# One step of a hybrid decoder layer on one core: q's opening, the widths of the product passes, and the products that follow a norm

## The chip, the core and the metric

The kernel runs on one core of a Trainium2 chip. Five engines work side by side: TensorE (PE in the profile, with PEld for its weight loads), VectorE (DVE), ScalarE (ACT), GpSimd (POOL) and SyncE (SP), which here issues nearly all DMAs. Each executes its own list of instructions in order; semaphores order them among each other. The metric is the time of one execution on the device, in microseconds (us).

## What is computed

One layer, applied to a prompt of 256 positions and to 8 samples of 4 new positions, 288 rows in all, in float32:

```
h   = RMSNorm(x)                                      x: 288 x 2048
q, k, v, u, v_g = split(h @ w_in)                     5 x 1024 columns; q and k with a partial rotary
A   = block-sparse attention (top 3 past blocks by q . mean(k), and the own block)
      the samples' past: 8 x 2048 positions in a paged cache of keys and values
B   = gelu(u) * (tril(W_s) @ LayerNorm(gelu(v_g)) + b)     in chunks of 128 positions
mix = (sigmoid(h Wg_a) * (A Wa) + sigmoid(h Wg_b) * (B Wb)) @ w_o
x   = x + RMSNorm(mix)
x   = x + RMSNorm((silu(a1) * g1) @ w_ffn_out),   a1, g1 = split(RMSNorm(x) @ w_ffn_in)    hidden width 5632
y   = x + (p @ w_ple) * sigmoid(RMSNorm(x) @ w_ple_gate)
```

## The kernel before, in words

**Layout.** Activations are kept transposed: a feature tile is 128 features on the partitions and T = 288 rows along the free dimension; x has KD = 16 tiles. A float32 product is made of three matmuls in a reduced float32 form. Weights are split into a high part `wh` (ScalarE, L224) and a low part `wl` (VectorE, L225), activations likewise into a pair of 288 + 288 columns (hh and hl in `hhl`, zh and zl in `zhl`, and so on). L228 multiplies wh with the high part, L229 wh with the low part, L230 wl with the high part.

**`product`** (L210) makes 256 output columns (two tiles t, two accumulators) over n feature tiles. It goes in chunks of four tiles k: one DMA of 512 KB into `wr` (WR = 4 buffers), a cast, a subtraction (three buffers each of wh and wl), then 24 matmuls ordered by (tile k, output tile t). In a chunk of fewer than four the order is by output tile first. With `wide` = 32 the first pass covers 320 columns, the second 256, and the 32 columns beyond T are added at the end through a small tile `rest` (L234, L235); with `wide` = 0 all three passes have 288. Only w_ffn_out's products set `wide`. A product is a generator that yields after each chunk; `weave` advances two of them in a given proportion.

**Opening** (L136 to L264). x comes in four DMAs of four tiles on SP's queue, q's weights beside them; gains and c_mix on ACT's queue, cst, the page table and kcst on POOL's. Ten matmuls on constants wake PE. Two of q's four products run together chunk by chunk as x arrives, behind them the sum of squares and `r0` (`r0_of`), the inverse root mean square of x. r0 multiplies the results of the products, not their inputs, so it is needed only at the first eviction. The other two products of q follow (L773). `rope` (L275) evicts q and k: a multiplication with r0 and four steps on 32 rows.

**Cache stage.** k, v, v_g, u and the gates' products follow, and the paged keys and values are scored between them. Every page is a DMA of 512 KB, preceded on SP by a read of its number in the page table (`page_load`, L553). Three big tiles of four pages each can be in flight; the first twelve pages can therefore be loaded before any score is made. In this stage, up to w_gate's last product, there are three "acc", two "long" and three "aux" banks of PSUM; afterwards six "acc" and two "aux".

**After the two norms.** mix and the FFN's output are normalised over all features: `norm_gap` puts small products of p with w_ple on PE while the norm's factor is computed. `residual` (L921) then walks over x in pairs of tiles: scale (L933), add to x (L935), split into zh (L937) and zl (L938), square (L940), add the squares up (L942, VectorE). The three first products of w_ffn_in, and of w_ple_gate, are woven in steps of chunks (L985, L1026); the residual as a whole stands ahead of them in the program. Their evictions need the factor of the next norm (r2, r3), which needs all squares.

**Tail.** Each product of w_ple_gate ends in four steps a tile (L1018 to L1021) and one DMA of two tiles to y.

**Order.** The order on each engine is not written out: a scheduler lists the instructions by their place in the program and by its own estimate of when their inputs are ready. `tc.issue_after(i)` forces an instruction behind another.

Of the kernel before, what the change touches and what calls it, by code (L numbers as in the profile page):

```python
# [42 lines left out]
WAKE, WR, BIG, PT, AUX, PB, LEAD, EG, LE, N1, N2, REST = 10, 4, 3, 1, 3, 2, 6, 2, 4, 20, 38, 325.0  # L43
# [40 lines left out]
def drain(gen):  # L84
    for _ in gen:
        pass
# [22 lines left out]
def tile_hybrid_step(ctx: ExitStack, tc: tile.TileContext, a: dict, o: list):  # L109
# [26 lines left out]
    def x_load(c):  # L136
        nc.sync.dma_start(xs[c], a["x"][:, c * XK:c * XK + XK])
# [17 lines left out]
    nc.gpsimd.dma_start(kcst, a["c_perm"][:, 128:])  # L155
# [30 lines left out]
    def h_parts(c):  # L186
        for i in range(XK):
            k = c * XK + i
            nc.scalar.activation(hh[:, k], xs[c][:, i], AF.Copy, scale=g_pre[:, k:k + 1])
            nc.vector.scalar_tensor_tensor(hl[:, k], xs[c][:, i], g_pre[:, k:k + 1], hh[:, k], op0=ALU.mult, op1=ALU.subtract)  # L190
# [16 lines left out]


    def product(w, c0, ks, part, done, name, of="acc", wide=0, hold=()):
# [4 lines left out]
        for k0 in range(0, n, 4):  # L214
            m = min(4, n - k0)
            raw = perm.tile([128, 4, GC], F32, name="wr", bufs=WR)
            r0 = ks[k0] * 128
            nc.sync.dma_start(raw[:, :m], w[r0:r0 + m * 128, c0:c0 + GC].rearrange("(k p) c -> p k c", p=128))
# [7 lines left out]
            for i, t in [(i, t) for i in range(m) for t in range(2)] if m == 4 else [(i, t) for t in range(2) for i in range(m)]:  # L226
# [4 lines left out]
            yield 0.74 * m  # L231
# [16 lines left out]
    def q_gen(g, of="acc"):  # L248
        yield from product(w_in, g * GC, K16, hpart, lambda x: rope(qT[:, 2 * g:2 * g + 2], x), "q", of)
# [14 lines left out]
    nc.scalar.dma_start(cm, a["c_mix"])  # L264
# [508 lines left out]
    for q in q2 + [q_gen(2), q_gen(3)]:  # L773
        drain(q)
# [306 lines left out]
```

## Time and profile before

| | us |
|---|---|
| median of 3 runs (lowest, highest) | 1820.64 (1820.21, 1822.02) |
| the profiled execution | 1820.68 |
| its span, first to last instruction | 1818.9 |

| Engine | busy us | share of the span |
|---|---|---|
| PE | 1798.5 | 99% |
| VectorE | 951.9 | 52% |
| ScalarE | 769.2 | 42% |
| GpSimd | 90.6 | 5% |

The granted TensorE clock is 0.996 of full on average. The DMA queues move 414.81 MB, 228 GB/s over the span; in the cache stage, up to about 700 us, they move 340 to 365 GB/s, afterwards about 165. Since matmuls are pipelined and their ends modelled, a busy PE tells nothing of its pace: a stage in which PE never stops is read by its number of matmuls and its length. Names in the rows such as fa, fg, f, o, pg are the accumulators of w_ffn_in's two halves, w_ffn_out, w_o and w_ple_gate.

### The profile page before, as it was taken

To read this page: it belongs to the slowest core of one execution; us is meant where nothing else is said; L and a number is where in the kernel's file an instruction comes from. 1 tells how busy PE (TensorE), PEld (TensorE's weight loads), DVE (VectorE), ACT (ScalarE), POOL (GpSimd) and SP (SyncE) were. 2 spreads that over 40 slices of the span, in tenths; PEclk is the share of its full clock that TensorE was granted. 3 is DMA by queue.
4 is the path that set the end of the run, shared out by engine and by line. 5 is a ranking of instruction groups with operands and counts; after the bars stand their busy time and mean duration, and the time that the engine had idled before them with its cause. 6 is when DMAs were issued, how large, how long until landed. Compare 5 with 4: busy or idle time off the path is not lost.

```text
span 1818.9 us, 38387 instructions
## 1 busy us (share of the span) xinstructions
PE 1798.5 (99%) x15818; PEld 1752.1 (96%) x15818; DVE 951.9 (52%) x1363; ACT 769.2 (42%) x1081; POOL 90.6 (5%) x169
## 2 busy tenths in 40 slices
PE   7999999999999999999999999999999999999998
PEld 7999899999999989999999999999999999999998
DVE  6654447544344346544854555434455554444774
ACT  5334465444333344445533333333333333444642
POOL 1010112000000000011000000000000000011000
PEclk9999999999999999999999999999999999999999
DMA  9589999999999995555555555455555555546363
GB/s 345 163 280 367 323 360 337 365 350 359 352 345 368 358 321 201 170 164 161 152 169 166 163 167 169 157 168 165 172 165 172 163 164 170 165 158 195 122 196 112
DMA packets 309136, 414.81 MB, mean 228 GB/s; under 512 B 13120, under 2 KB 273344, under 8 KB 308832
## 3 DMA queue, kind: packets, MB, share of 16 engines
q1 hardware_dynamic: 307728, 409.16, 67.0%
q8 instruction: 124, 2.03, 0.5%
q0 software_dynamic: 944, 2.79, 0.4%
q10 hardware_dynamic: 288, 0.41, 0.1%
q14 instruction: 52, 0.43, 0.1%
HBM read 407.45 MB, written 4.85 MB: 227 GB/s over the span
## 4 chain that ended last, share of the span: by engine, by line
PE 94%; DVE 3%; DMA 1%; SPq 1%; issue 1%; ACT 1%; DVEq 0%; ACTq 0%
PE f L228 6%; PE f L230 5%; PE fg L228 5%; PE fg L230 5%; PE fg L229 5%; PE fa L230 5%; PE fa L228 5%; PE fa L229 5%; PE f L229 5%; PE values L696 3%; PE scores L598 3%; PE gb L228 2%; PE ga L228 2%; PE gb L230 2%; PE o L228 2%; PE o L230 2%
## 5 line engine op out<-in xcount | busy, mean ns | idle before, releaser
L225 DVE TENSOR_TENSOR wl<-wr,wh 128x1024 fp32r<-128x1024 f32 x512 | 618.8, 1209 | 708.2 <-ACT wh L224 704.4
L224 ACT CAST wh<-wr 128x1024 fp32r<-128x1024 f32 x512 | 530.9, 1038 | 881.0 <-PE f L229 140.4
L228 PE MATMUL f<-dhl,wh 128*128 128x320 f32 x704 | 217.1, 308 | 0.0
L229 PE MATMUL fg<-zhl,wh 128*128 128x288 f32 x704 | 208.2, 296 | 0.0
L230 PE MATMUL fa<-zhl,wl 128*128 128x288 f32 x704 | 206.8, 295 | 1.2 <-DVE wl L225 1.2
L229 PE MATMUL fa<-zhl,wh 128*128 128x288 f32 x704 | 207.9, 296 | 0.0
L228 PE MATMUL fg<-zhl,wh 128*128 128x288 f32 x704 | 207.3, 295 | 0.2 <-ACT wh L224 0.2
L230 PE MATMUL fg<-zhl,wl 128*128 128x288 f32 x704 | 207.0, 295 | 0.0
L230 PE MATMUL f<-dhl,wl 128*128 128x288 f32 x704 | 207.0, 294 | 0.0
L228 PE MATMUL fa<-zhl,wh 128*128 128x288 f32 x704 | 206.3, 296 | 0.1
L229 PE MATMUL f<-dhl,wh 128*128 128x256 f32 x704 | 196.6, 279 | 0.0
L230 PEld LDWEIGHTS fa<-zhl,wl 128*128 128x128 f32 x704 | 133.3, 189 | 1.4 <-DVE wl L225 1.4
L230 PEld LDWEIGHTS fg<-zhl,wl 128*128 128x128 f32 x704 | 133.3, 190 | 0.0
L229 PEld LDWEIGHTS f<-dhl,wh 128*128 128x128 f32 x704 | 132.4, 188 | 0.0
L228 PEld LDWEIGHTS fg<-zhl,wh 128*128 128x128 f32 x704 | 132.1, 188 | 0.4 <-ACT wh L224 0.4
L229 PEld LDWEIGHTS fa<-zhl,wh 128*128 128x128 f32 x704 | 132.4, 188 | 0.1
L229 PEld LDWEIGHTS fg<-zhl,wh 128*128 128x128 f32 x704 | 132.3, 188 | 0.0
L228 PEld LDWEIGHTS fa<-zhl,wh 128*128 128x128 f32 x704 | 131.6, 188 | 0.7 <-ACT zhl L937 0.4
L230 PEld LDWEIGHTS f<-dhl,wl 128*128 128x128 f32 x704 | 132.2, 188 | 0.0
L228 PEld LDWEIGHTS f<-dhl,wh 128*128 128x128 f32 x704 | 132.0, 188 | 0.0
L228 PE MATMUL gb<-hhl,wh 128*128 128x288 f32 x256 | 76.7, 300 | 0.0
L228 PE MATMUL ga<-hhl,wh 128*128 128x288 f32 x256 | 76.5, 299 | 0.0
(327 smaller groups left out, 3740.6 us busy)
## 6 DMA issues: line engine op xcount, KB each, us to landing
wr<-in_w_ffn_in SPq DMA_DIRECT2D x176, 512.0 KB, 3.7
kt<-in_cache_k SPq DMA_DIRECT2D x128, 512.0 KB, 7.7
vt<-in_cache_v SPq DMA_DIRECT2D x128, 512.0 KB, 6.6
wr<-in_w_in SPq DMA_DIRECT2D x80, 512.0 KB, 7.2
wr<-in_w_ffn_out SPq DMA_DIRECT2D x80, 512.0 KB, 3.4
wr<-in_w_gate SPq DMA_DIRECT2D x64, 512.0 KB, 7.4
wr<-in_w_o SPq DMA_DIRECT2D x32, 512.0 KB, 3.5
wr<-in_w_ple_gate SPq DMA_DIRECT2D x32, 512.0 KB, 3.5
```

Of the source, the lines that this page charges most:

```text
L224: nc.scalar.copy(wh[:, :m], raw[:, :m])
L225: nc.vector.tensor_tensor(wl[:, :m], raw[:, :m], wh[:, :m], ALU.subtract)
L228: nc.tensor.matmul(accs[t], wh[:, i, c], x[:, :T + wide], start=k == 0, stop=False)
L229: nc.tensor.matmul(accs[t][:, wide:T], wh[:, i, c], x[:, T + wide:], start=False, stop=False)
L230: late["mm"] = nc.tensor.matmul(accs[t][:, :T], wl[:, i, c], x[:, :T], start=False, stop=k == n - 1)
L598: i = nc.tensor.matmul(sp[b][32 * g:32 * g + 32, 4 * n:4 * n + 4], Q[:, h2, g, dq], kt[:, :, c:c + 32], start=h2 == 1 and dq == 0, stop=h2 ...
L696: i = nc.tensor.matmul(oa[b][32 * g:32 * g + 8], w[:, n, 32 * g + 8 * part:32 * g + 8 * part + 8], v[:, :, g], start=first and part == 3, ...
```

## The change

- **Opening.** x comes in pieces of tiles (0,1), (1,2), (2,4), (4,8), (8,12), (12,16), the second on ACT's queue. Three products of q run together over these pieces, in banks "acc", "long" and "aux"; for pieces of fewer than four tiles the weights have buffers of their own (`w1`, `w2`). `r0_of` now stands ahead of the third product's last chunk, behind the last matmul before it. cst, kcst and c_mix move to SP's queue, behind weight loads 11 and 13. Each of the first twelve pages (FIRST) is issued only after weight load 9 + n. Eight wake matmuls in place of ten.
- **Products.** `wide` is 32 everywhere: passes of 320, 256 and 288 columns. The last chunk of every product is ordered by output tile first.
- **After the norms.** The first three products yield after each tile (`fine`), and `first_products` advances the residual by one pair for every two tiles of the first product, four tiles ahead at the start. The squares' sums are taken out of the residual's loop and made in one go (`norm_of_squares`) once all pairs have been put out.
- **Tail.** The last tile's four steps are made in two halves of 144 columns, and the last two tiles of y have a DMA each.

```diff
-WAKE, WR, BIG, PT, AUX, PB, LEAD, EG, LE, N1, N2, REST = 10, 4, 3, 1, 3, 2, 6, 2, 4, 20, 38, 325.0
+WAKE, FIRST, WR, BIG, PT, AUX, PB, LEAD, EG, LE, N1, N2, REST = 8, 12, 4, 3, 1, 3, 2, 6, 2, 4, 20, 38, 325.0
...
-    def x_load(c):
-        nc.sync.dma_start(xs[c], a["x"][:, c * XK:c * XK + XK])
+    pieces = [(0, 1), (1, 2), (2, 4)] + [(k, k + XK) for k in range(XK, KD, XK)]
+
+    def x_load(k0, k1):
+        (nc.scalar if k0 == 1 else nc.sync).dma_start(xs[k0 // XK][:, k0 % XK:k0 % XK + k1 - k0], a["x"][:, k0:k1])
...
-    x_load(0)
+    x_load(*pieces[0])
+    x_load(*pieces[1])
     cst = perm.tile([128, 128], F32, name="cst")
-    nc.gpsimd.dma_start(cst, a["c_perm"][:, :128])
...
-    nc.gpsimd.dma_start(kcst, a["c_perm"][:, 128:])
...
-    def product(w, c0, ks, part, done, name, of="acc", wide=0, hold=()):
+    def product(w, c0, ks, part, done, name, of="acc", wide=32, cuts=None, hold=(), fine=False):
...
-        for k0 in range(0, n, 4):
-            m = min(4, n - k0)
-            raw = perm.tile([128, 4, GC], F32, name="wr", bufs=WR)
+        for k0, k1 in cuts or [(k, min(k + 4, n)) for k in range(0, n, 4)]:
+            m = k1 - k0
+            if cuts and m < 4:
+                raw = p_x0.tile([128, m, GC], F32, name=f"w{m}", bufs=6 // m)
+            else:
+                raw = perm.tile([128, 4, GC], F32, name="wr", bufs=WR)
...
-            for i, t in [(i, t) for i in range(m) for t in range(2)] if m == 4 else [(i, t) for t in range(2) for i in range(m)]:
+            steps = [(i, t) for i in range(m) for t in range(2)]
+            for i, t in sorted(steps, key=lambda s: s[1]) if k1 == n else steps:
...
-            yield 0.74 * m
+                if fine and t and k1 < n:
+                    yield 0.74
+            if not fine or k1 == n:
+                yield 0.74 * m
...
-    q2 = [q_gen(0), q_gen(1, "long")]
-    for c in range(KD // XK):
-        h_parts(c)
-        for q in q2:
+    q3 = [q_gen(g, of, pieces) for g, of in enumerate(("acc", "long", "aux"))]
+    for i, (k0, k1) in enumerate(pieces):
+        h_parts(k0, k1)
+        for q in q3:
+            if k1 == KD and q is q3[2]:
+                squares(k1 // XK - 1)
+                with tc.issue_after(late["mm"].ins):
+                    r0_of()
             next(q)
-        if c + 1 < KD // XK:
-            x_load(c + 1)
-        squares(c)
-    r0_of()
+        if 1 < i + 1 < len(pieces):
+            x_load(*pieces[i + 1])
+        if k1 % XK == 0 and k1 < KD:
+            squares(k1 // XK - 1)
+    with tc.issue_after(loads[11].ins):
+        nc.sync.dma_start(cst, a["c_perm"][:, :128])
+        nc.sync.dma_start(kcst, a["c_perm"][:, 128:])
...
-    nc.scalar.dma_start(cm, a["c_mix"])
+    with tc.issue_after(loads[13].ins):
+        nc.sync.dma_start(cm, a["c_mix"])
...
+            if len(issued) < FIRST:
+                st.enter_context(tc.issue_after(loads[9 + len(issued)].ins))
...
-            if m:
-                nc.vector.tensor_tensor(src[:, 0:2], src[:, 0:2], src[:, s], ALU.add)
+            yield
+
+    def norm_of_squares(src, key):
+        for m in range(2, KD, 2):
+            nc.vector.tensor_tensor(src[:, 0:2], src[:, 0:2], src[:, m:m + 2], ALU.add)
         ssq[key] = [src[:, 0], src[:, 1]]
+        return norm_of(key)
+
+    def first_products(ps, src, rstd, g_next):
+        res = residual(src, rstd, g_next)
+        drain(islice(res, 2))
+        for i, _ in enumerate(weave(weave(ps[0], 1.0, ps[1], 1.0), 2.0, ps[2], 1.0)):
+            if i % 2:
+                next(res, None)
+            if i == 11:
+                yield
...
-            drain(weave(weave(pairs[0], 1.0, pairs[1], 1.0), 2.0, pairs[2], 1.0))
+            first = first_products(pairs[:3], mo_f, r1, g_pf)
+            next(first)
+            r2 = norm_of_squares(mo_f, "x1")
...
+            drain(first)
...
-            nc.vector.tensor_tensor(gt, x[t], r3, ALU.mult)
...
+            for c in (slice(0, T // 2), slice(T // 2, T)) if m == KD - 1 else (slice(0, T),):
+                nc.vector.tensor_tensor(gt[:, c], x[t][:, c], r3[:, c], ALU.mult)
...
+            if g == 7:
+                nc.sync.dma_start(y_o[:, m], x1[:, m])
```

## Rows read from the trace of the kernel before

**Rows 1.** The page, part 1: engine, busy us (share of span), instructions.

```profile
PE 1798.5 (99%) x15818; PEld 1752.1 (96%) x15818; DVE 951.9 (52%) x1363; ACT 769.2 (42%) x1081; POOL 90.6 (5%) x169
```

**Rows 2.** View of waits, PE: what waited for what; us, times, longest.

```profile
PE q L228 <- ACT wh L224: 6.3, 2, 3.8
PE q L230 <- DVE wl L225: 2.5, 3, 1.6
...
PE fa L230 <- DVE wl L225: 1.2, 1, 1.2
```

**Rows 3.** Timeline of PE: start us, us, instruction, count, [idle before <- releaser].

```profile
9.54 0.61 PE L228 MATMUL q<-hhl,wh 128*128 128x288 f32 x1 [3.84 <-ACT wh L224]
...
72.47 0.29 PE L228 MATMUL k<-hhl,wh 128*128 128x288 f32 x1
```

**Rows 4.** Windows of w_o, w_ffn_in, w_ffn_out: length, busy (count) by engine, clock, DMA.

```profile
750.00:846.00 96.00, 96.00 (x728) 96.00 (x727) 41.58 (x38) 45.70 (x65) 14.92 (x13) 1.00 0.56 180
...
1275.00:1555.00 280.00, 280.00 (x2114) 280.00 (x2113) 141.47 (x174) 108.58 (x135) 0.00 (x0) 1.00 0.54 167
1562.00:1696.00 134.00, 134.00 (x1018) 134.00 (x1017) 62.40 (x81) 61.71 (x95) 16.93 (x13) 1.00 0.55 175
```

**Rows 5.** Timeline of SP's issues in the opening.

```profile
1.21 0.97 SPq L218 DMA_DIRECT2D wr<-in_w_in  x2
...
25.36 4.98 SPq L560 DMA_DIRECT2D kt<-in_cache_k  x4
31.60 6.26 SPq L218 DMA_DIRECT2D wr<-in_w_in  x4
```

**Rows 6.** DMA view from 0.5, 12, 31, 52: KB, us to landing.

```profile
x<-in_x SPq DMA_DIRECT2D x1, 576.0 KB, 4.6
...
DMA packets 3533, 7.40 MB, mean 390 GB/s; under 512 B 219, under 2 KB 2275, under 8 KB 3532
...
wr<-in_w_in SPq DMA_DIRECT2D x3, 512.0 KB, 9.8
...
wr<-in_w_in SPq DMA_DIRECT2D x4, 512.0 KB, 3.6
```

**Rows 7.** Window 45 to 50 us; after POOL's come clock, DMA share and GB/s.

```profile
45.00:50.00 5.00, 5.00 (x21) 5.00 (x22) 2.89 (x3) 0.50 (x2) 0.00 (x0) 0.50 0.65 189
```

**Rows 8.** Timeline of ACT and DVE, 5 to 9 us.

```profile
5.52 1.81 ACT L189 ACTIVATE hhl<-x,gains 128x288 fp32r<-128x288 f32 x4 [2.83 <-DMA gains<-in_gains]
...
7.26 0.43 DVE L567 COPY spread<-cst 128x512 f32<-128x512 f32 x1 [6.25 <-DMA cst<-in_c_perm]
```

**Rows 9.** Groups of DVE by line, 28 to 72.4 us: busy us, mean ns.

```profile
L278 DVE TENSOR_TENSOR A<-q,r 128x288 f32<-128x288 f32 x7 | 2.9, 450 | 1.2 <-PE q L230 1.2
...
L281 DVE TENSOR_TENSOR rope<-rope,cm 32x576 f32<-32x576 f32 x3 | 2.2, 744 | 0.1
```

**Rows 10.** View of tile rest, 1270 to 1700 us: ns min/median/max.

```profile
L234 ACT COPY rest<-f x18: 172/174/187, 1279.6 to 1699.7; 128x32 f32<-128x32 f32 x18
L235 DVE TENSOR_TENSOR f<-f,rest x18: 191/193/200, 1280.9 to 1699.9; 128x32 f32<-128x32 f32 x18
```

**Rows 11.** Groups of DVE by line, 854.3 to 889 us.

```profile
L225 DVE TENSOR_TENSOR wl<-wr,wh 128x1024 fp32r<-128x1024 f32 x9 | 11.0, 1228 | 0.0
L938 DVE SCALAR_TENSOR_TENSOR zhl<-x,gains,zhl 128x288 fp32r<-128x288 f32 x16 | 8.1, 520 | 0.1
...
L942 DVE TENSOR_TENSOR mo_f<-mo_f 128x576 f32<-128x576 f32 x7 | 5.3, 761 | 0.0
```

**Rows 12.** Timeline of ACT behind the first norm.

```profile
866.44 2.95 ACT L224 CAST wh<-wr 128x1024 fp32r<-128x1024 f32 x3 [0.63 <-ACT mo_f L940]
```

**Rows 13.** Timeline of DVE and SP in the tail.

```profile
1812.93 0.85 DVE L1018 TENSOR_TENSOR pgt<-pg,r_x 128x288 f32<-128x288 f32 x2 [6.90 <-PE pg L230]
...
1815.52 0.36 SPq L1022 DMA_DIRECT2D out<-x  x1
```

**Rows 14.** Window of u's products in the cache stage.

```profile
325.00:397.00 72.00, 72.00 (x843) 67.18 (x842) 36.95 (x70) 30.92 (x43) 4.08 (x13) 1.00 1.02 365
```

More of the change, by code (lines that the diff above doesn't have):

```diff
@@ L771, in cache_gen @@
         products()
-    for q in q2 + [q_gen(2), q_gen(3)]:
+    for q in q3 + [q_gen(3)]:
         drain(q)
@@ L919, in tile_hybrid_step, with residual @@
     zh, zl = zhl[:, :, :T], zhl[:, :, T:]
-    def residual(src, rstd, g_next, key):
+    def residual(src, rstd, g_next):
         last, adds = [], []
@@ L982, in tile_hybrid_step @@
             hold = [late["sq"]] if half == 0 and g == 1 else []
-            pairs += [product(w_fi, c0, K16, zpart, done_a, "fa", hold=hold), product(w_fi, FF + c0, K16, zpart, done_g, "fg")]
+            pairs += [product(w_fi, c0, K16, zpart, done_a, "fa", hold=hold, fine=half == 0 and g < 2),
+                      product(w_fi, FF + c0, K16, zpart, done_g, "fg", fine=half == 0 and g < 1)]
         if half == 0:
-            drain(weave(weave(pairs[0], 1.0, pairs[1], 1.0), 2.0, pairs[2], 1.0))
+            first = first_products(pairs[:3], mo_f, r1, g_pf)
+            next(first)
+            r2 = norm_of_squares(mo_f, "x1")
+            end_m.close()
+            p_f, end_f = pool("p_f", "left")
+            dhl = p_f.tile([128, HT, 2 * T], F32R, name="dhl", tag="dh")
+            dh, dl = dhl[:, :, :T], dhl[:, :, T:]
+            fo = p_f.tile([128, KD, T], F32, name="fo")
+            drain(first)
         for p in pairs:
@@ L1017, in pg_done @@
             gt = p_f.tile([128, T], F32, name="pgt", tag="fs", bufs=4)
-            nc.vector.tensor_tensor(gt, x[t], r3, ALU.mult)
-            nc.scalar.activation(gt, gt, AF.Sigmoid)
-            nc.vector.tensor_tensor(gt, gt, le[:, m], ALU.mult)
-            nc.vector.tensor_tensor(x1[:, m], x1[:, m], gt, ALU.add)
-        nc.sync.dma_start(y_o[:, 2 * g:2 * g + 2], x1[:, 2 * g:2 * g + 2])
-    pg = [product(w_pg, g * GC, K16, zpart, lambda x, g=g: pg_done(x, g), "pg",
-                  hold=[late["sq"], late["fo"]] if g == 2 else []) for g in range(8)]
-    drain(weave(weave(pg[0], 1.0, pg[1], 1.0), 2.0, pg[2], 1.0))
+            for c in (slice(0, T // 2), slice(T // 2, T)) if m == KD - 1 else (slice(0, T),):
+                nc.vector.tensor_tensor(gt[:, c], x[t][:, c], r3[:, c], ALU.mult)
+                nc.scalar.activation(gt[:, c], gt[:, c], AF.Sigmoid)
+                nc.vector.tensor_tensor(gt[:, c], gt[:, c], le[:, m, c], ALU.mult)
+                nc.vector.tensor_tensor(x1[:, m, c], x1[:, m, c], gt[:, c], ALU.add)
+            if g == 7:
+                nc.sync.dma_start(y_o[:, m], x1[:, m])
+        if g < 7:
+            nc.sync.dma_start(y_o[:, 2 * g:2 * g + 2], x1[:, 2 * g:2 * g + 2])
+    pg = [product(w_pg, g * GC, K16, zpart, lambda x, g=g: pg_done(x, g), "pg",
+                  hold=[late["sq"], late["fo"]] if g == 2 else [], fine=g < 3) for g in range(8)]
+    first = first_products(pg[:3], fo, r4, g_pl)
+    next(first)
+    r3 = norm_of_squares(fo, "x2")
+    drain(first)
     for p in pg[3:]:
```

28 lines of the change are left out of this document (10 added, 18 removed).

## The prediction

> **What bounds the kernel now.** I first read the page's busy shares: TensorE (PE) is busy 99% of the span [rows 1]. So I ask two things only: where PE still waits, and at what pace it streams. The view of waits, PE alone, answers the first: in 1818.9 us PE waits 8.8 us in q's opening and 1.2 us where w_ffn_in begins after a norm (the same again where w_ple_gate begins); the other waits are under 1.2 us each [rows 2]. Two stretches don't show up there in full: the time before q's first matmul at 9.54 us [rows 3], and the tail after the last matmul. The windows answer the second question: in the stages of w_o, w_ffn_in and w_ffn_out PE never stops, so a stage's time is the number of its matmuls times their pitch [rows 4].
>
> The profiled execution took 1820.68 us (span 1818.9 and 1.8 around it), the median of three runs is 1820.64; so the sum is made against 1820.68 and needs no correction.
>
> **Opening, the largest term.** q's 384 matmuls and the 4 of r0 run from 9.54 us to k's first at 72.47 [rows 3], 62.9 us. At the pitch of w_o's window, (728 - 2)/96 us or 132.2 ns each [rows 4], 384 take 50.8 and r0's about 0.8; 11.3 us are lost inside, 9.5 before. The loss inside: the twelve first pages of the cache (kt) stand in one queue with q's weights. SP issues four kt loads from 25.36 us, and the first weights of q's third product only at 31.60 [rows 5]; these need 9.8 us to land, 3.6 when the queue is short [rows 6]. PE then waits for a cast of those weights and for their low part (6.3 and 2.5 us with the start [rows 2]), and after these waits the granted clock is 0.50 from 45 to 50 us, the lower of its two levels [rows 7].
>
> The change does four things to it.
> (a) The first piece needs one tile of x (144 KB) and weight pieces of 128 KB in place of 576 and 512. Now x needs 4.6 us from its issue at 0.76 to landing [rows 6], gains are there at 5.52, and VectorE stands at `spread` until 7.26, waiting for `cst`, with hl behind it [rows 8]. With `cst` behind load 11, `spread` can't hold up hl at 7 us; should it stand in VectorE's order ahead of `cst`'s landing, it holds up a wl later, which I price with the losses below. One tile of x lands 432 KB or 1.1 us (at 390 GB/s [rows 6]) sooner, at 4.2; gains between that and 5.5. I take 5.0. Then hh 0.45 (a quarter of 1.81 [rows 8]), hl about 0.5 (zl, the same form, has 0.52 [rows 11]; the 320-column pass reads both), and hops: first matmul at 6.0, ends 5.2 and 7.0. Two wakes fewer end the wake sooner, for an opening that starts sooner.
> (b) Three products use each tile of x, so PE has more work to each byte of x; and page n now stands behind load 9 + n, one page to a load. In the stretch of loads 9 to 17 come 9 loads, 9 pages, half of x and 0.65 MB of constants: 18 x 0.524 + 1.18 + 0.65 = 11.3 MB, 29 us at the 390 GB/s that the queue gave when it was full [rows 6]. PE's work on these loads is 216 x 0.1322 = 28.6 us. The queue keeps pace with no slack but its head start: 0.5 us of waits, with 0 and 6 as ends.
> (c) More DMAs are issued: 9 pieces of weights and 6 of x for what took 5 loads and 4 of x. SP issues two in 0.97 us [rows 5], so eight extra are 4 us of SP, spread over 13 us of PE's work on the pieces: piece 1 is issued by 3.6 us, and PE wants it at 8.4. The smaller casts carry a fixed share each: bounded by a quarter and two fifths of a four-tile cast (1.0 to 1.2 us [rows 11, 12]) ACT and VectorE have at most 3 x 0.5 + 0.5 = 2.0 us for a tile, against PE's 18 x 0.132 = 2.4. The second and third casts still come one after the other at the start: 1.5 us. POOL loses two issues and ACT one; SP's three for constants stand behind loads 11 and 13, ahead of pages and later loads, and their bytes are in the sum of (b).
> (d) r0 now comes at the end: its matmuls stand behind the second product's last, and rope of all three products waits for it. A rope is 2 x 0.45 + 4 x 0.74 = 3.9 us on VectorE [rows 9], 11.7 for three; q's last product needs 4 wl of 1.2 us in the same 13 us. That is 16.6 us of work on an engine that runs in order, and a wl queued behind rope makes PE wait: 0 (two wl are done before r0) to 3.6; I take 1.5.
> Sum: 6.0 + 50.8 + 0.8 + 0.5 + 1.5 + 1.5 = 61.1 us for 72.5: **-11.4 us**, ends -5 and -15. Everything behind starts relative to q's end, pages too, so the shift is kept.
>
> **Passes of 320, 256, 288.** Still three matmuls and 864 columns; but w_ffn_out has these widths already. Its window gives (1018 - 2) in 134 us, 131.9 ns a matmul; w_ffn_in's (2114 - 2) in 280, 132.6; w_o's 132.2 [rows 4]. So 0.7 ns on 4224 matmuls of w_ffn_in, 3.0 us, and about 0.35 on the other 5760, 2.0 us: **-5.0 us**, ends 0 and -7. Each of 112 products gains two copies of 0.17 us on ACT and two adds of 0.19 on VectorE [rows 10], about 40 us on either; in w_ffn_in's window they are busy 109 and 141 of 280 us [rows 4], so it costs PE nothing while a bank is free. The last chunk tile by tile gives the first accumulator 1.6 us (12 matmuls) more for that and moves no work: 0.
> By the Trainium skill (TensorE: Matmul & The Clock Gate, Back-to-back issue gap) a warm matmul costs its columns at 2.4 GHz and 2.5 ns more, so three passes of 864 columns cost the same however they are cut, and this term would be 0. The trace's 132.2 ns for 288 columns lies 9.7 above that figure, so something else is in the pitch, and the rule need not hold for it; its result is rival B.
>
> **Products woven after the two norms.** From 854 to 889 us VectorE has no gap: 9 wl (11.0 us), 16 zl (8.1), 7 adds of squares (5.3), and the residual's scalings and sums [rows 11]. Three woven products use up their three wh buffers together, so casts for all three start in a row at 866.44 [rows 12], and the first wl behind them stands after such adds. PE loses about 2.5 us in each of the two places by the start times of its matmuls (1.2 as one wait [rows 2], shorter ones around it). The change takes the adds out of the stretch up to the last tile and lets the third product advance at half the pace, so that its buffer comes free at another time. There are still three buffers for three products: a cast and a wl (2.3 us) lie between a freed buffer and its next use. The third product's 24 matmuls (3.2 us) cover that if they are put there. I take 1.7 off each place: **-3.4 us**, ends 0 and -5. The norm's result comes behind the adds, near 891 us as now; PE needs a bank from it at 896. The chain before the first zl is untouched.
>
> **Tail.** Now VectorE multiplies from 1812.93, the last DMA is issued at 1815.52 [rows 13], and the span ends 3.4 us later. After: tile 14 is done early; tile 15 first needs a copy and an add (0.17 + 0.19 [rows 10]), then four steps in halves, 0.5 + 1.9 us against 2.6 now; half the bytes may land 0.1 sooner. **-0.3 us**, ends +0.4 and -1.
>
> **Sum:** 1820.68 - 11.4 - 5.0 - 3.4 - 0.3 = 1800.6 us.
>
> **Rivals.**
> A, the queue still starves the opening. 29 us of transfers in 28.6 of work leaves no slack, and one late load brings the lower clock as now. Then (b) and (d) cost 8.4 us for 2.0: 1807.0. For it: 9.8 us to landing [rows 6]; against: pages are held one to a load. Chance 0.15.
> B, the widths give nothing: w_o and w_ffn_in have the same widths and differ by 0.4 ns [rows 4], so other operands alone can make such a difference. 1805.6. Chance 0.20.
> C, slower: up to the end of the cache's stage there are three "acc" banks, and a product's second tile needs the bank of the previous first tile 2.0 us after that tile's end. A copy behind a cast of 1.05 us, an add behind a wl of 1.23, then the multiply: up to 3.1 us. 40 products follow each other there (k, v, g, u 4 each, gb, b, ga 8). It decides from 20.1/40 = 0.5 us each; at 1.0 it gives 1840.6, and the DMA engines, all busy there (share 1.02 [rows 14]), make nothing up. Against it: the budget is 0.8 us now, and no wait of PE on an eviction shows. Chance 0.08.
> D, the weave doesn't do what it says: three buffers still free up in one row, and PE waits for wh as it did for wl. 1804.0. Chance 0.12.
>
> **How the numbers follow.** The forecast keeps 0.45. Its own ends with A, B and D reach from about 1793 to 1812; outside lie C and a mixture of all of A, B and D at 1815. A measurement of this kernel can tell 0.2% (3.6 us), so faster means under 1817.0: all but C and a little beyond the mixture. Faster 0.88, within 0.2% 0.04, slower 0.08.
>
> **What would show it.** q's first matmul near 6 us and k's near 61; no window of the opening at a granted clock of 0.50; w_ffn_in's window at 131.9 ns a matmul, not 132.6; no wait of 1.2 us for wl after either norm; no gap before a product's second tile between 61 and 690 us. It is wrong if k starts after 67 us, if w_ffn_in keeps its pitch, or if such gaps appear.

## The result, and the profile after

The changed kernel takes 1802.68 us (median of 5, 1799.92 to 1804.71), the kernel before in the same series 1820.30 us (5 executions). The ratio is 0.9904, 95% interval 0.9889 to 0.9918: 1.0% faster. The forecast was 1800.6 us with a range of 1793 to 1812. The profiled execution of the changed kernel took 1802.68 us, its span is 1800.91, so 18.0 us of span have gone.

The page of the kernel after, part 1 (engine, busy us, share of the span, instructions; compare [rows 1]):

```profile
PE 1783.9 (99%) x15814; PEld 1738.8 (97%) x15814; DVE 985.0 (55%) x1596; ACT 799.2 (44%) x1312; POOL 82.2 (5%) x167
```

PE is still busy 99% of the span. ACT and DVE have 30 and 33 us more to do, mainly for the small tile `rest`, and POOL has 8 us less. So as before only two things can be read: where PE waits, and its pace, to which its granted clock belongs. The view of waits of the kernel after, PE alone (what waited for what: us, times, longest):

```profile
PE pg L238 <- DVE wl L232: 2.1, 1, 2.1
PE fa L236 <- DVE zhl L960: 1.5, 1, 1.5
PE pg L236 <- DVE zhl L960: 1.5, 1, 1.5
PE q L236 <- DVE hhl L191: 1.5, 1, 1.5
...
PE q L236 <- ACT wh L231: 0.9, 1, 0.9
PE q L238 <- DVE wl L232: 0.9, 2, 0.5
PE gb L236 <- DVE eg L414: 0.4, 1, 0.4
PE fa L238 <- DVE wl L232: 0.3, 1, 0.3
```

Against [rows 2]: q's waits have fallen from 8.8 to 3.3 us. The 1.2 us for `wl` has shrunk to 0.3 in w_ffn_in's first products, but has grown to 2.1 in w_ple_gate's. And the first matmul behind each norm now waits 1.5 us for the low half of `zhl`; before, w_ple_gate's first matmul waited 0.9 us for the high half, and w_ffn_in's had no wait in the view. Windows of the kernel after, in w_o, w_ffn_in and w_ffn_out (length, busy and count of PE, PEld, DVE, ACT, POOL, then clock, DMA share, GB/s), to set against [rows 4]:

```profile
737.00:833.00 96.00, 96.00 (x731) 96.00 (x730) 43.84 (x55) 48.06 (x80) 11.10 (x13) 1.00 0.57 179
1260.00:1535.00 275.00, 275.00 (x2100) 275.00 (x2099) 147.28 (x216) 112.38 (x177) 0.00 (x0) 1.00 0.55 168
1546.00:1676.00 130.00, 130.00 (x988) 130.00 (x987) 60.72 (x78) 59.40 (x93) 17.06 (x13) 1.00 0.55 176
```

The pitch is (731 - 2) in 96 us or 131.7 ns in w_o (132.2 before), (2100 - 2) in 275 or 131.1 in w_ffn_in (132.6 before), and 131.8 in w_ffn_out (131.9 before, with the same widths then).

By the starts of PE's matmuls the span is cut into stages, each from its first matmul to the next one's; w_ffn_out ends at the start of its last matmul, where the next stretch begins.

| Stretch | before, us | after, us | difference |
|---|---|---|---|
| start of the span to q | 9.54 | 4.61 | -4.93 |
| q to k | 62.93 | 56.62 | -6.31 |
| k to w_o's first matmul (cache stage, then the products into a) | 675.58 | 673.64 | -1.94 |
| w_o | 101.60 | 101.26 | -0.34 |
| le to w_ffn_out, first half (norm, w_ffn_in) | 291.31 | 288.74 | -2.57 |
| w_ffn_out, first half | 139.09 | 139.11 | 0.0 |
| w_ffn_in, second half | 280.17 | 277.03 | -3.14 |
| w_ffn_out, second half | 139.11 | 139.11 | 0.0 |
| its end to w_ple_gate's first | 9.00 | 9.57 | +0.57 |
| w_ple_gate, to its last matmul | 104.66 | 105.61 | +0.95 |
| tail | 5.92 | 5.60 | -0.32 |

The opening brings 11.2 us, the cache stage 1.9, w_o and w_ffn_in about 6, the tail 0.3; the end of the FFN and w_ple_gate, where the norm's weave should have helped, have lost 1.5.

### The profile page after: what moved, and what is told of

Read it like the earlier page. It is cut to its first block, busy times and chain, and to the rows that moved or that the text cites. A ratio compares the mean times of both kernels' runs of the same rounds, so it can differ in the third digit from the quotient of the medians.

```text
span 1800.9 us, 38860 instructions
## 1 busy us (share of the span) xinstructions
PE 1783.9 (99%) x15814; PEld 1738.8 (97%) x15814; DVE 985.0 (55%) x1596; ACT 799.2 (44%) x1312; POOL 82.2 (5%) x167
## 4 chain that ended last, share of the span: by engine, by line
PE 95%; DVE 2%; DMA 1%; ACT 0%; issue 0%; SPq 0%; DVEq 0%; ACTq 0%
PE fg L236 6%; PE fa L236 6%; PE f L236 6%; PE f L238 5%; PE fa L238 5%; PE fg L238 5%; PE f L237 5%; PE fg L237 5%; PE fa L237 5%; PE values L717 3%; PE scores L619 3%; PE ga L236 2%; PE o L236 2%; PE gb L236 2%; PE ga L238 2%; PE o L238 2%
## 5 line engine op out<-in xcount | busy, mean ns | idle before, releaser
L232 DVE TENSOR_TENSOR wl<-wr,wh 128x1024 fp32r<-128x1024 f32 (+1 forms) x509 | 615.1, 1209 | 700.5 <-ACT wh L231 692.1
L231 ACT CAST wh<-wr 128x1024 fp32r<-128x1024 f32 (+1 forms) x509 | 526.4, 1035 | 745.8 <-issue 174.5
L236 PE MATMUL fa<-zhl,wh 128*128 128x320 f32 x704 | 218.9, 311 | 1.6 <-DVE zhl L960 1.5
L236 PE MATMUL fg<-zhl,wh 128*128 128x320 f32 x704 | 218.9, 311 | 0.0
L237 PE MATMUL fg<-zhl,wh 128*128 128x256 f32 x704 | 196.4, 279 | 0.0
L237 PE MATMUL fa<-zhl,wh 128*128 128x256 f32 x704 | 196.4, 279 | 0.0
L236 PEld LDWEIGHTS fa<-zhl,wh 128*128 128x128 f32 x704 | 132.2, 188 | 2.1 <-DVE zhl L960 1.7
L238 PEld LDWEIGHTS fa<-zhl,wl 128*128 128x128 f32 x704 | 131.9, 188 | 0.6 <-DVE wl L232 0.5
L236 PEld LDWEIGHTS fg<-zhl,wh 128*128 128x128 f32 x704 | 132.2, 188 | 0.2
L238 PEld LDWEIGHTS f<-dhl,wl 128*128 128x128 f32 x704 | 132.2, 188 | 0.0
L237 PEld LDWEIGHTS fa<-zhl,wh 128*128 128x128 f32 x704 | 132.2, 188 | 0.0
L237 PEld LDWEIGHTS fg<-zhl,wh 128*128 128x128 f32 x704 | 132.2, 188 | 0.0
L236 PE MATMUL pg<-zhl,wh 128*128 128x320 f32 x256 | 79.8, 314 | 1.5 <-DVE zhl L960 1.5
L236 PE MATMUL gb<-hhl,wh 128*128 128x320 f32 x256 | 79.9, 314 | 0.4 <-DVE eg L414 0.4
```

What stands on the lines that cost most here:

```text
L231: nc.scalar.copy(wh[:, :m], raw[:, :m])
L232: nc.vector.tensor_tensor(wl[:, :m], raw[:, :m], wh[:, :m], ALU.subtract)
L236: nc.tensor.matmul(accs[t], wh[:, i, c], x[:, :T + wide], start=k == 0, stop=False)
L237: nc.tensor.matmul(accs[t][:, wide:T], wh[:, i, c], x[:, T + wide:], start=False, stop=False)
L238: late["mm"] = nc.tensor.matmul(accs[t][:, :T], wl[:, i, c], x[:, :T], start=False, stop=k == n - 1)
```

## Experiments

Where a kernel ran once (e3, e4, e5, e6, e7, e10) it is read by the lengths of its stages and not by its total: the same opening varies by 1.8 us from execution to execution. The length of a stage needs TensorE's granted clock beside it. Windows of the opening (length, busy and count of PE, PEld, DVE, ACT, POOL, then clock, DMA share, GB/s), first e6, whose opening is word for word that of the changed kernel, then the changed kernel:

```profile
32.00:36.00 4.00, 3.62 (x17) 3.62 (x18) 1.55 (x2) 1.49 (x2) 0.00 (x0) 0.57 1.06 373
32.00:36.00 4.00, 3.94 (x30) 3.94 (x31) 1.23 (x2) 1.83 (x2) 0.00 (x0) 1.00 1.07 373
```

In e6 the clock fell for a while to the lower of its two levels (0.50, 1.2 GHz) behind the waits at weight load 13, in the changed kernel's profiled execution it stayed at 1.00 (2.4 GHz). The same two outcomes stand behind the wait of 2.1 us in w_ple_gate, first the changed kernel, then e7, which has the same products, weave and wait there:

```profile
1703.80:1707.20 3.40, 3.40 (x17) 3.40 (x16) 3.40 (x6) 0.99 (x2) 0.00 (x0) 0.52 0.85 278
1701.40:1704.80 3.40, 3.40 (x28) 3.40 (x27) 3.40 (x6) 1.18 (x2) 0.00 (x0) 1.00 0.85 282
```

With the lower clock w_ple_gate takes 105.61 us; e7 takes 104.07, and e3, where the clock held too, 104.04. So some 1.5 of the 105.61 us are the lower clock's, which came behind this wait in one execution and not in the others; a comparison with the changed kernel's w_ple_gate has to set them aside.

**e1: the opening alone**, on the products, order, norms and tail of before. Against the changed kernel:

```diff
-    def product(w, c0, ks, part, done, name, of="acc", wide=32, cuts=None, hold=(), fine=False):
+    def product(w, c0, ks, part, done, name, of="acc", wide=0, cuts=None, hold=(), fine=False):
...
-            for i, t in sorted(steps, key=lambda s: s[1]) if k1 == n else steps:
+            for i, t in sorted(steps, key=lambda s: s[1]) if m < 4 and not cuts else steps:
...
-        drain(islice(res, 2))
-        for i, _ in enumerate(weave(weave(ps[0], 1.0, ps[1], 1.0), 2.0, ps[2], 1.0)):
+        drain(res)
+        yield
+        drain(weave(weave(ps[0], 1.0, ps[1], 1.0), 2.0, ps[2], 1.0))
```

> The kernel before with the new opening alone (pieces of x, three products of q together, r0 at the end, constants and pages behind weight loads, eight wakes); widths, order of the last chunk, the products after the norms and the tail are as before. Theory: the opening is worth what the two traces show up to k's first matmul, 72.47 against 61.23 us, and nothing behind it gives any of it back, since all later work starts relative to q's end: k's first matmul at 61.2 +- 1 us, the median 11.2 us under the kernel before (about 1809.3 against 1820.5), each stage from k to the end within 0.3 us of its old length. Rival: the cache stage, with its DMA engines all busy, gives some of it back: k at 61 us, but the first matmul of w_a_out less than 9 us earlier than before, the median above 1812.

1807.85 us (median of 4) against 1819.52: ratio 0.9934 [0.9917, 0.9950], -11.7 us. In its profiled execution q starts at 4.51 and k at 62.85, 9.6 us sooner than [rows 3] and later than the 61.2 +- 1 that were expected: here the clock fell in the opening (0.50 from 34 to 36 us). w_o's first product starts 10.7 us sooner and the span ends 12.3 us sooner; the stages behind k are up to 1.1 us shorter, where 0.3 was expected. So the shift is kept through the whole cache stage, and by the medians the opening is worth what the forecast gave it.

**e2: the widths alone**, on the kernel before (the edit's other line only drops the `wide=32` that w_ffn_out's products had named).

```diff
-    def product(w, c0, ks, part, done, name, of="acc", wide=0, hold=()):
+    def product(w, c0, ks, part, done, name, of="acc", wide=32, hold=()):
```

> The kernel before with passes of 320, 256, 288 columns in all products, nothing else: old opening, last chunk ordered by feature tile, residual and woven products as before. Theory: the widths alone make w_ffn_in's pitch 131.1 ns a matmul (132.6 before, 131.1 with the whole change), 9 to 10 us over all products; they cost 1.9 us at the first tile after the two norms, because the first pass now waits for zl; and with the old order an accumulator's copy and add have 0.8 us where a bank is shared, so there are short waits in the cache stage, a few us in sum: median 1812 to 1817. Rival 1: the pitch comes from the order of the last chunk, not from the widths: 132.6 ns, median 1820 or more. Rival 2 (the one of the prediction that ends slower): waits on banks of 0.5 us and more at each of 40 products: cache stage 20 us longer, median above 1830.

1810.50 us (4) against 1819.52: ratio 0.9952 [0.9935, 0.9969], -9.0 us, more than any side expected. Window of w_ffn_in and waits of PE:

```profile
1275.00:1545.00 270.00, 270.00 (x2062) 270.00 (x2061) 143.86 (x214) 110.35 (x171) 0.00 (x0) 1.00 0.55 169
```

```profile
PE fa L228 <- DVE zhl L938: 1.5, 1, 1.5
PE pg L228 <- DVE zhl L938: 1.5, 1, 1.5
```

(2062 - 2) in 270 us is 131.1 ns: the widths alone give the new pitch, so rival B is out. No wait for a bank appears between k and ga, so C is out too. And the two waits for `zhl` are here without any change to the norms: the first pass now reads 32 columns of zl, which the pass of 288 columns didn't. The first tile costs 1.35 us (le to fa, 9.44 for 8.09) and 0.57 us (9.57 for 9.00). Up to v's first matmul the profiled execution is 1.9 us ahead (4.3 in the opening, which has the old order of loads and the same lower clock behind its waits, less 2.4 in k), which isn't put down to the widths; from there to the end it gains 8.6 us, and that is the figure taken for the widths below.

**e3: the old order of the last chunk**, all else as after.

```diff
-            for i, t in sorted(steps, key=lambda s: s[1]) if k1 == n else steps:
+            for i, t in sorted(steps, key=lambda s: s[1]) if m < 4 and not cuts else steps:
```

> The changed kernel with the old order in the last chunk (by feature tile in place of output tile first), nothing else. Theory: the order moves no pitch; its worth is the 1.6 us that it gives the first accumulator's copy and add while three banks are shared. Without it the cache stage (k's first to w_a_out's first matmul, 623.0 us with the whole change) gets 5 to 15 us longer, by gaps of 0.2 to 0.4 us before a product's second tile; w_ffn_in keeps 131.1 ns. One time 1808 to 1818. Rival: the scheduler has slack enough without it, as it had for a chain of 0.8 us before: cache stage within 1 us of 623.0, one time 1801 to 1805.

1800.30 us in its one execution. The cache stage, k's first to w_a_out's first matmul, takes 621.38 us for 623.01: not 5 to 15 us longer, as was expected, but 1.6 shorter. Stage gb takes 37.73 us for 38.67, ga 132.90 for 132.50, the tail 6.02 for 5.60. (w_ple_gate takes 104.04 for 105.61, but that is the clock: e7, with the new order, takes 104.07.) The order, which was forecast at 0, has small costs and small gains, of about 1 us at most, and costs 1.2 us in all here (1.6 from k to w_o, less 0.4 in the tail); gb's is the surest of them, since it took 38.66 to 38.68 in every kernel with 320 columns and the new order, and 37.71 to 37.73 in those with the old one.

**e4: other widths**, 352, 224, 288 and 304, 272, 288.

```diff
-    def product(w, c0, ks, part, done, name, of="acc", wide=32, cuts=None, hold=(), fine=False):
+    def product(w, c0, ks, part, done, name, of="acc", wide=64, cuts=None, hold=(), fine=False):
```

> The changed kernel with passes of 352, 224 and 288 columns in place of 320, 256, 288; 864 columns as ever. Three theories of the pitch of w_ffn_in, 132.6 ns with three equal passes and 131.1 with 320, 256, 288, where the gain sits in the third pass (132.3 to 128.4 ns). W1, the operands and not the widths set it: 131 ns again, one time within 2 us of 1802.7. W2, a pass is cheaper behind a shorter one: the third pass falls further, pitch 130 to 130.6, one time 1790 to 1797. W3, a pass of 224 columns is over before the next weights are in: the second pass stays at 116 ns or more in place of 104, pitch 133 or more, one time above 1815.

> The changed kernel with passes of 304, 272 and 288 columns. Measured so far in w_ffn_in, for the same 864 columns: 132.6 ns a matmul with three equal passes, 131.1 with 320, 256, 288, 135.8 with 352, 224, 288. Theory: a third pass gets cheaper behind a shorter second one, until the second is too short; then 16 columns give half of what 32 give, 131.7 to 132.0 ns, w_ffn_in's second half 278.3 to 279 us in place of 277.0, one time 1804 to 1807. Rival: the gain doesn't follow the length of the second pass: 131.1 ns or 132.6 as at one of the two neighbours.

1847.62 us with 64, 1818.25 with 16 (`wide=16` in the same line). Windows of w_ffn_in, first with 64, then with 16:

```profile
1320.00:1575.00 255.00, 255.00 (x1883) 255.00 (x1882) 134.97 (x199) 101.61 (x158) 0.00 (x0) 1.00 0.52 162
```

```profile
1280.00:1550.00 270.00, 270.00 (x2038) 270.00 (x2038) 142.46 (x211) 108.49 (x169) 0.00 (x0) 1.00 0.54 166
```

The number of matmuls and of columns is the same in all four; the pitch in w_ffn_in is 132.6 ns for 288, 288, 288 [rows 4], 132.6 for 304, 272, 288, 131.1 for 320, 256, 288 and 135.6 for 352, 224, 288. It neither stays constant nor falls with the step. From start to start, on average in these windows, the three passes take 132, 134, 132 ns; 141, 125, 132; 149, 116, 128; and 161, 104, 142. So with 16 and 32 the wide pass pays for its columns and the narrow one gives them back, and at 32 the third pass, whose 288 columns haven't changed, is 4 ns shorter; at 64 it is 10 ns longer. The theory of a steady gain with the step fell. Pitch and time with 64 came as W3 expected, but not by its mechanism: the second pass does fall to 104 ns, and the first and the third are longer. What shortens or lengthens the third pass was not found.

**e5: equal widths in the woven products alone** (the first three of w_ffn_in, where the same is added, and of w_ple_gate).

```diff
-                  hold=[late["sq"], late["fo"]] if g == 2 else [], fine=g < 3) for g in range(8)]
+                  hold=[late["sq"], late["fo"]] if g == 2 else [], fine=g < 3, wide=0 if g < 3 else 32) for g in range(8)]
```

> The changed kernel, but the three woven products after each norm have three passes of 288 columns; all other products keep 320, 256, 288. Theory: the first pass of 320 columns reads zl of the first tile as well as zh, which costs 1.35 us behind the first norm (8.09 to 9.44 us from the first small product to w_ffn_in's first matmul) and 0.57 behind the second (9.00 to 9.57). With 288 columns both come back, 8.1 and 9.0 us; six products of 112 lose 1.1 to 1.5 ns a matmul, 0.7 us. One time 1 to 1.5 us under the changed kernel, 1800 to 1803; and the stretch that follows gives some of it back if VectorE, not PE, sets it: then w_ffn_in's first half is 1.3 us longer than its 279.3, and nothing is won. Rival: the first tile's wait is not the width's: 9.4 and 9.6 us as they are.

1800.32 us. The first tile comes 0.56 us sooner in both places (8.88 for 9.44, 9.01 for 9.57), w_ple_gate takes 103.64 us for 105.61, w_ffn_in's first half 279.99 for 279.31. So the pass of 320 columns costs 0.56 us at each first tile of the new weave, and the first products of w_ffn_in lose as much again in pitch as they gain; in w_ple_gate and its first tile there is a net gain of 2.5 us, of which 1.5 is the clock (it held here), and the wait of 2.1 us for `wl` isn't among its waits.

**e6: the old residual and weave**, all else as after.

```diff
-            yield
-
-    def norm_of_squares(src, key):
-        for m in range(2, KD, 2):
-            nc.vector.tensor_tensor(src[:, 0:2], src[:, 0:2], src[:, m:m + 2], ALU.add)
+            if m:
+                nc.vector.tensor_tensor(src[:, 0:2], src[:, 0:2], src[:, s], ALU.add)
...
-        drain(islice(res, 2))
-        for i, _ in enumerate(weave(weave(ps[0], 1.0, ps[1], 1.0), 2.0, ps[2], 1.0)):
+        drain(res)
+        yield
+        drain(weave(weave(ps[0], 1.0, ps[1], 1.0), 2.0, ps[2], 1.0))
```

> The changed kernel with the products after the norms as before: residual put out whole ahead of them, sums of squares inside its loop, weave by chunks of four tiles. Theory (rival D of the prediction): the new weave is worth nothing, since the scheduler lists instructions by readiness and wove by feature tile already, the sums of squares still run between the tiles, and three casts still start in a row; w_ffn_in's first half stays within 0.6 us of 279.3, w_ple_gate's stage gets shorter than its 105.6 us, 103.4 to 104.6. One time 1800 to 1803. Rival (the prediction's term): the weave saves 1.7 us in each place: 281.0 and 107.3 us, one time 1806.

1801.64 us. From fa to w_ffn_out 279.81 us (after 279.31), w_ple_gate 103.39 (after 105.61). The new weave gains 0.5 us at the first norm and loses 2.2 at the second, 1.7 us net on the wrong side. Of the 2.2, 1.5 are the lower clock: against e7 and e3, which have the new weave and the full clock there, the loss is 0.7, and the two norms together come to +0.2. The waits of e6:

```profile
PE pg L238 <- DVE wl L232: 1.3, 1, 1.3
PE fa L238 <- DVE wl L232: 1.3, 1, 1.3
```

These are the 1.2 us of [rows 2] in both places; the weave has taken one away and made the other 2.1. Timeline of DVE in the kernel after, where PE waits at the second norm (start, us, instruction), and of PE there:

```profile
1697.08 0.75 DVE L968 TENSOR_TENSOR fo<-fo 128x576 f32<-128x576 f32 x1
...
1699.27 0.75 DVE L957 TENSOR_TENSOR x<-x,fo 128x576 f32<-128x576 f32 x1
1699.94 0.75 DVE L968 TENSOR_TENSOR fo<-fo 128x576 f32<-128x576 f32 x1
1700.61 0.75 DVE L957 TENSOR_TENSOR x<-x,fo 128x576 f32<-128x576 f32 x1
1701.28 2.35 DVE L232 TENSOR_TENSOR wl<-wr,wh 128x1024 fp32r<-128x1024 f32 x2
```

```profile
1702.55 0.53 PE L238 MATMUL pg<-zhl,wl 128*128 128x288 f32 x2 [2.07 <-DVE wl L232]
```

L968 is the sum of squares. The program text puts all of them behind the last pair; in the order of DVE they still stand between the pairs, because each is ready as soon as its square is, and the scheduler lists by readiness. The `wl` that PE wants stands behind two of them (the first `wh` of that row is cast from 1697.11 on, so the sum at 1699.94 stands between it and its `wl`). This opening, word for word that of after, took 58.37 us from q to k, for 56.62, with the lower clock from 32 us on that is shown above.

**e7: pages four loads later.**

```diff
-                st.enter_context(tc.issue_after(loads[9 + len(issued)].ins))
+                st.enter_context(tc.issue_after(loads[13 + len(issued)].ins))
```

> The changed kernel with page n behind weight load 13 + n in place of 9 + n. Theory: the queue bounds the opening: four pages lie ahead of load 13, which lands at 29.6 us and makes PE wait 0.94 us for its cast and 0.46 for wl. With the pages four loads later, load 13 lands by 25 us, PE's waits after 20 us vanish, k's first matmul comes 1 to 1.5 us sooner, at 59.8 to 60.3 us; the pages are not needed before the first scores, 31 us later. One time 1801 to 1803 with all else kept. Rival: the total of bytes bounds the opening, not their order, and the wait moves to a later load: k's first at 61 us as now.

1798.68 us; q to k takes 53.91 us, k starts at 58.54, better than expected. Timeline of SP's issues, first after, then e7:

```profile
16.05 3.98 SPq L581 DMA_DIRECT2D kt<-in_cache_k  x4
20.92 0.39 SPq L225 DMA_DIRECT2D wr<-in_w_in  x1
```

```profile
16.80 0.38 SPq L225 DMA_DIRECT2D wr<-in_w_in  x1
18.27 0.36 SPq L581 DMA_DIRECT2D kt<-in_cache_k  x1
```

In the changed kernel loads 9 to 12 have all been issued by 16 us, so the first four pages go out in one row after all, ahead of load 13. That load lands at 29.6 us; with four pages (2.1 MB, 5.4 us at the 390 GB/s of [rows 6]) out of its way it lands at 24.2. PE's waits in q then are one of 0.5 us, where after has 3.3. Of the 2.7 us gained from q to k, 2.1 lie behind the last matmul ahead of the wait at load 13; the rest comes before it, where PE waits for pieces of x and their weights and the executions with the pages unmoved differ by 1.1 us, so that part isn't shown to be the pages'. No wait at load 13 also means no lower clock behind it: in e7, e11 and e12 the clock holds through the whole opening, and these take 53.5 to 53.9 us. The forecast's "one page to a load" is true of e7 and not of the first four pages of the change.

**e10: the sums of squares forced behind the last zl.**

```diff
+                    late["zl"] = last[-1]
...
         for m in range(2, KD, 2):
-            nc.vector.tensor_tensor(src[:, 0:2], src[:, 0:2], src[:, m:m + 2], ALU.add)
+            with tc.issue_after(late["zl"].ins):
+                nc.vector.tensor_tensor(src[:, 0:2], src[:, 0:2], src[:, m:m + 2], ALU.add)
```

> The changed kernel with each of the seven sums of squares forced behind the last zl of the residual. Theory: in the changed kernel three of them (0.76 us each) still stand ahead of the first wl of the second chunks, and PE waits there, 0.3 us after the first norm and 2.1 after the second. Without them that wl is done 2.2 us sooner and the wait after the second norm vanishes: w_ple_gate's stage 103.5 us in place of 105.6, w_ffn_in's first half 279.0 for 279.3. One time 1800 to 1802. Rival: the casts in a row (three buffers for three products) hold PE, not the sums: stage lengths unchanged within 0.5 us; or the norm's result, now later by up to 3 us, makes PE wait for a bank: 106 us or more.

1800.69 us; w_ple_gate takes 102.56 us for 105.61, and 0.8 less than with the old weave (e6). Against the new weave at the full clock (e7, 104.07) the forced order gains 1.5 us; the rest of the 3.05 is the clock, which held here behind a wait of 0.6. Timelines of DVE and PE in e10, for the same place:

```profile
1698.98 1.43 DVE L957 TENSOR_TENSOR x<-x,fo 128x576 f32<-128x576 f32 x2
1700.31 1.23 DVE L232 TENSOR_TENSOR wl<-wr,wh 128x1024 fp32r<-128x1024 f32 x1
...
1701.60 0.53 PE L238 MATMUL pg<-zhl,wl 128*128 128x288 f32 x2 [0.62 <-DVE wl L232]
```

No L968 stands there any more, and `wl` starts 9.6 us behind w_ple_gate's first matmul, for 11.6. The wait falls from 2.07 to 0.62 us, as much as the stage gains at the full clock. From fa to w_ffn_out it is 279.34 us, for 279.31: the first norm gains nothing. So the sums were what made the weave's wait at the second norm.

**e11: e7 and e10 together**, and **e12: with the old order of the last chunk besides**, except in w_ple_gate's last product.

```diff
-            for i, t in sorted(steps, key=lambda s: s[1]) if k1 == n else steps:
+            for i, t in sorted(steps, key=lambda s: s[1]) if k1 == n and (m < 4 or last) else steps:
```

> The changed kernel with two edits together: pages behind load 13 + n, and the sums of squares forced behind the last zl. Theory: they act in different stages and add up: opening 53.9 us for 56.6 to 58.4, w_ple_gate's stage 102.6 for 105.6. Median 1795 to 1797.5, ratio to the kernel before 0.986 to 0.9875. Rival: the opening's 53.9 us was the luck of one run, as the same opening took 56.6 and 58.4 us in other runs: median 1798.5 to 1800.

> The same two edits, and the last chunks ordered by feature tile again, but for w_ple_gate's last product. Theory: the order by output tile costs more than it gives: it took 0.95 us in v_g's stage and 0.94 in the first gate's stage (a gap of 0.8 us in one place), gave 0.4 in w_gate's second stage, and its 0.4 in the tail is kept here. Median 1 to 2 us under the run with two edits. Rival: those stages vary by as much from run to run, and the two medians agree within 0.5 us.

e11 takes 1797.18 us (4) against 1819.73: ratio 0.9876 [0.9859, 0.9894]. q to k is 53.52, w_ple_gate 102.56, as in e7 and e10 (0.3 us is lost between, from fa to w_ffn_out 279.63 for 279.31). Its four executions lie within 0.2 us at a mean granted clock of 0.999 to 1.000; the changed kernel's five lie within 4.8, and the two longest of them, 1804.35 and 1804.71, have 0.997 where the others have 0.999. e12 takes 1796.26 (4; 1795.60 to 1797.13): 0.9873 [0.9855, 0.9890]. It is 0.9 us under e11, on the same chip, but the intervals overlap, so that the order costs something is likely and not shown by the times; by stages e12 gains 1.67 in g and 0.95 in gb and gives back 1.01 in ga. e12 is the fastest of all, and 6.4 us under the changed kernel by the medians of their two series.

## Why the prediction was right, and where it was not

The total was forecast at -20.1 us and came at -18.0 in the profiled execution. Its terms fared differently:

| Term | forecast | measured | from |
|---|---|---|---|
| opening | -11.4 | -11.2 | k's start, [rows 3] against 61.23 |
| widths | -5.0 | -8.6 from v on | e2 against before, by stages |
| woven norms | -3.4 | +0.2 | e6 against after (first norm) and e7 (second) |
| lower clock in w_ple_gate | none | +1.5 | after against e7 and e3 |
| order of last chunks | 0 | about +1 | e3 without w_ple_gate, e12 |
| tail | -0.3 | -0.3 | 5.60 for 5.92 |

**Opening: right in size, by two errors that cancel.** (a) q's first matmul was forecast at 6.0 us, ends 5.2 and 7.0; it came at 4.61. The step that failed is "I take 5.0" for the gains. Timeline of ACT after: the cast starts at 3.38, once the gains are in, for 5.52 in [rows 8].

```profile
3.38 0.54 ACT L190 ACTIVATE hhl<-x,gains 128x288 fp32r<-128x288 f32 x1 [0.20 <-DMA gains<-in_gains]
```

The losses inside were forecast at 3.5 us beyond PE's work of 51.6; they are 56.62 - 51.6 = 5.0, of which the view of waits shows 3.3. Timeline of PE after, the places where it waits:

```profile
11.35 0.41 PE L236 MATMUL q<-hhl,wh 128*128 128x320 f32 x1 [1.47 <-DVE hhl L191]
17.45 0.53 PE L238 MATMUL q<-hhl,wl 128*128 128x288 f32 x2 [0.47 <-DVE wl L232]
30.80 0.42 PE L236 MATMUL q<-hhl,wh 128*128 128x320 f32 x1 [0.94 <-ACT wh L231]
32.06 0.54 PE L238 MATMUL q<-hhl,wl 128*128 128x288 f32 x2 [0.46 <-DVE wl L232]
```

Part (c) put 1.5 us on casts that come one after the other at the start. A wait of 1.5 us is there, but at the third piece, whose hl comes late because its x does: it lands at 9.81 us, and ACT waits for it (timeline of ACT after):

```profile
9.83 0.96 ACT L190 ACTIVATE hhl<-x,gains 128x288 fp32r<-128x288 f32 x2 [1.89 <-DMA x<-in_x]
```

In e3 and e7, with the same pieces, x is there at 8.4 and 8.6 and PE doesn't wait for it. That the figure agrees is luck. Part (b), the queue, was priced at 0.5 and costs 0.94 + 0.46 us at load 13 in waits alone; e7 shows that the order of the pages was worth 2.1 us from there on. So the sum of bytes against work (29 us in 28.6) was a fair account of the mean and blind to the four pages that go in a row. Part (d), 1.5 us for rope and r0, shows no wait: nothing in q's waits stands behind the third product's last load. Rival A's mechanism, a late load that brings the lower clock, came true in four of the eight executions with this order of pages (e1, e6, e10 and e4 with 16): the clock fell behind load 13, and q to k took 58.3 to 59.9 us, for 56.6 to 57.2 in the other four. Its price of 6.4 us was too high. That the changed kernel's profiled execution is one of the four without it is luck, and the forecast's sign "no window of the opening at a granted clock of 0.50" holds for that execution and not for this opening. Window of the kernel after from 45 to 50 us, against [rows 7]:

```profile
45.00:50.00 5.00, 5.00 (x38) 4.89 (x38) 3.96 (x7) 3.37 (x6) 0.00 (x0) 1.00 1.05 372
```

The granted clock is 1.00 (2.4 GHz) where it was 0.50 (1.2 GHz) behind the waits of [rows 2]; 38 matmuls stand in these 5 us for 21.

**Widths: the mechanism right, the size off.** The pitch in w_ffn_in fell to 131.1 ns, not to the 131.9 that was borrowed from w_ffn_out's window: 1.5 ns x 4224 = 6.3 us for 3.0. (The -8.6 of e2 is net of 1.9 us lost at the first tiles and 0.7 in its tail.) The step that failed is that a pitch belongs to the widths: w_ffn_out, w_o and w_ffn_in have the same three widths after the change and run at 131.8, 131.7 and 131.1 ns, as they differed before. The Trainium skill (TensorE: Matmul & The Clock Gate, Back-to-back issue gap) gives a warm matmul its columns at 2.4 GHz and 2.5 ns more, by which equal columns would cost the same however they are cut; the section adds that this is the gap of a single matmul by itself and miscounts in a stream of weight loads and matmuls, which the prediction left out. The runs here differ by up to 4.5 ns a matmul between two cuts (131.1 and 135.6, e4), so the measurement decides against the rule for this stream.

**First tile behind a norm: a sentence that was wrong.** "The chain before the first zl is untouched" is true of the norm's code and missed that the wider pass reads zl where the old one read zh alone: 1.35 and 0.57 us (e2), with the old norms; the forecast had used that very fact, "the 320-column pass reads both", in the opening.

**Woven norms: failed.** "Takes the adds out of the stretch up to the last tile" was read off the program's text. The order on DVE is the scheduler's, and the adds stayed (DVE after, second norm, above). Rival D's mechanism was right in part: behind the first norm the third product's slower pace didn't part the buffers, three casts still start in one row there (two behind the second norm), but PE waits for `wl` and not for `wh`. Timeline of ACT after, as [rows 12]:

```profile
853.66 2.95 ACT L231 CAST wh<-wr 128x1024 fp32r<-128x1024 f32 x3 [0.58 <-ACT mo_f L962]
```

Rival D was priced as the loss of the gain (0), and that is what the weave itself comes to: +0.2 us, with 1.5 more where the clock fell behind its wait, which the prediction hadn't priced. A fourth pair of weight buffers would show what the buffers alone cost; it was not tried, so their part is open. e10 shows the adds' share at the second norm, 1.5 us at the full clock.

**Order and tail.** The order was forecast to move no work and to cost nothing; e3 and e12 put it at about 1 us. The tail came as forecast: halves of 144 columns, and the copy and add of `rest`.

**C** was not seen: the longest wait on another engine between k and ga is 0.4 us, for `eg`.

The widths gave 3.6 us more than forecast; the norms gave 3.6 less, the clock took 1.5 and the order about 1. So the total missed by 2.1 us only, and that is luck too. The measured terms add up to -17.2 (with 1.2 for the order) of the 18.0; the 0.8 us left are within what the opening alone varies by. A total that comes out says little on its parts; e1, e2 and e6 do.

## What to carry to other kernels

Where a scheduler orders the engines, moving statements in the program isn't moving instructions: look for the moved line in the trace, and force the order where it matters (e10 had 1.5 us from one forced order, and 3 with the clock that no longer fell). In a shared queue, not the mean rate but what stands directly ahead of the next needed load decides; a rule "one page behind each load" whose first loads have already gone lets several pages out at once. A pitch read from one product is no pitch for another with the same widths; measure it there, and check who reads the extra columns of a widened pass. Before two executions are compared by the length of a stage, set the granted clock of that stage beside it: here one fall of the clock behind a short wait was worth as much as most of the edits.

## What the runs showed of the hardware

- Three passes of 864 columns in all, each with a weight load of its own, took 397.8 ns (288, 288, 288), 397.8 (304, 272, 288), 393.4 (320, 256, 288) and 406.7 (352, 224, 288) in w_ffn_in. The minimum lies at one split and not at the end of the series. Why isn't known.
- The same opening took 56.58, 56.62, 56.88, 58.28 and 58.37 us from q to k in five executions of kernels with that opening unchanged (e5, after, e3, e10, e6), and 53.5 to 53.9 in the three with later pages. In the three shorter ones the granted clock stays at 1.00, in the two longer ones it falls to 0.50 behind the waits at load 13: the 60 matmuls behind the first of them take 10.3 and 10.2 us, for 8.7 to 8.8.
- The same wait doesn't always bring the lower clock. Behind 2.0 to 2.1 us for `wl` in w_ple_gate it fell in the changed kernel and in e4 with 16, and held in e3 and e7. At load 13 PE waited 1.7 us in e5 and the clock held, 1.6 in e6 and e10 and it fell. What decides isn't shown.
- q's first matmul started 4.5 to 4.8 us after the start of the span with 144 KB of x and 128 KB of weights; it was 9.54 with 576 and 512 KB.
